# A four-branch mixer layer: the HGRN and GLA tiles issued two at a time, and the mLSTM gate rows in the mixers' banks

## The chip, the cores and the metric

The kernel runs on one core of one Trainium2 chip. The metric is device microseconds of one launch. A core has five engines, each with its own instruction stream that is executed in order: PE multiplies matrices, DVE and POOL do elementwise work and scans, ACT does activations and copies, and SP issues the DMA transfers. An engine waits at the head of its stream until what that instruction needs is there; nothing behind it can pass.

## The reference, cut to what matters

One layer (DEPTH 1) over 2048 tokens of width 1024, in float32: four causal mixers read the same normalised input, and their outputs are gated and summed.

```python
def gla_chunkwise(q, k, v, log_g):      # branches C (HGRN2, 4 heads) and D (GLA, 4 heads)
    ...                                 # chunk by chunk:
    # o = tril(q k^T with decay ratios) v + (q * decay) @ state
    # state = decay_last * state + (k * rest of the decay)^T v
...
def mlstm_chunkwise(q, k, v, log_i, log_f):   # branch B
    ...
    b = jnp.cumsum(fc, axis=-1)
    Dm = jnp.where(mask, b[..., :, None] - b[..., None, :] + ic[..., None, :], -jnp.inf)
...
y = x + (sum over branches of sigmoid(gate_i) * (mixer_i @ W_i)) @ W_out
```

In branches C and D each channel has a decay of its own at each token, so the products between tokens of a chunk can't be one plain matrix product; the kernel builds them level by level (blocks of 8, then 8, 16, 32 and 64 tokens against their neighbours).

## The kernel before, in words

The sequence is worked through in two halves of 1024 tokens. Each half goes through the same stages: the input is normalised and split into high and low parts; `ahead_pairs` runs the large projections (`product`, matmuls at L428) and between them, by the table GORD, the RG-LRU and the mLSTM; `mixers` (L1212) runs the HGRN and GLA recurrences; `merge` and `outp` gate, sum and project the result. In the profiled execution the mixers' stage of the first half lies at about 830 to 1210 us, that of the second at about 2210 to 2580 us.

`mixers` has twelve tiles of 512 tokens: for j in 0 to 3 one HGRN head each, for j = 4 and 5 two GLA heads each, and each j in two parts gi = 0 and 1, the second of which takes up the state S[j] that the first leaves. They are written one after the other, (0,0), (0,1), (1,0) and so on. A tile is the generator `gla_tile` (L977), in eight steps between its `yield`s. It makes a scan Gc of the log decays (L987), an 8-token scan g8 (L989), weights from them (POOL L992, ACT L993 and L994, DVE L995 and L996), the products within blocks of 32 (the 32x32 matmuls of `diag`, L1012, masked at L1020); then for each level of 8, 16, 32 and 64 tokens two POOL subtractions (L1031, L1032), one ACT exponential (L1033), two DVE products (L1034, L1035), and the matmuls (L1012 for the two small levels, L1055 for the two large ones) with their evictions (L1038, L1060). After that come the transposes of the weighted keys (L1078), the state (L1084, L1091), the outputs (L1100, L1104), the norm (ACT L1114 to L1122), transposes back (L1126), the gate product (DVE L1127) and the store (SP, L1130).

PE has other work to do beside the tiles: `ip_vals` (matmuls at L285 into the two banks pb, evicted by ACT at L1145 and DVE at L1147, by DVE at L1149 for the low-rank gate) makes the values that the tiles need, and `gates_ahead` (matmuls at L273) makes merge gates ahead of their time, as many before each tile as the table FILL says. I call the two filler. The weights of filler are split into high and low parts by ACT L254 and POOL L255.

What sets the order: the program is written once, and a scheduler gives each instruction a priority by its place in the program. Tiles are written under `prio(MIX)`, which places them 4000 ahead of filler written at the same place; evictions and weight splits of filler are placed 6000 ahead. The scheduler then lays out each engine's stream with an estimate of its own of when each instruction can start, the highest priority among those ready first. That order is fixed in the program; the chip doesn't change it. Buffers matter too: SBUF slots are handed out by a ring in program order, so that a later tile's slot can be one that an earlier tile has yet to give up. Two ring lists hand out PSUM banks: `bank()` turns over the mixers' banks mx (mx[3:] while the mLSTM runs beside the projections, all six of them in the mixers), `bank8()` those that the projections use (pb and mx[:3] at that time). The mLSTM's gate rows, `mlstm_rows`, take two of their banks (pg, pt) from `bank8()`.

Of the kernel before, what the change touches and what calls it, by code (L numbers as in the profile page):

```python
# [28 lines left out]
NPB = 2  # L29
NG = 10  # L30
PRE = (("mx", 4), ("mo", 4), ("mz", 4), ("hq", 4), ("hz", 4), ("gz", 4), ("gq", 2), ("gk", 2))
LIM = 10
NTH = 0
RMS = 0
NW = 6
NR = 4
# [5 lines left out]
GORD = [('g',2),('r',1),('z',1),('g',1),('z',1),('r',1),('g',1),('z',2),('r',1),('g',1),('z',2),('r',1),('z',6),('t',0),('m',0),('g',1),('m',0),('g',1),('m',0),('c',2),('g',1),('m',0),('c',4),('d',0),('m',0),('c',4),('g',1),('c',5),('g',1),('c',5),('d',1),('c',5),('g',1),('c',5),('g',1),('c',5),('g',1),('c',5),('z',1),('c',4),('z',1),('c',4)]  # L42
NORM = {"hz": "hnw", "gz": "gnw"}
SILU = ("lz", "mz", "hq", "hz", "gz")
FILL = [0, 2, 0, 0, 0, 1, 0, 0, 1, 0, 0, 0, 2, 0]


PV = {}
# [99 lines left out]
class Trunk:  # L148
# [49 lines left out]
    def free(self, *aps):  # L198
        self.ar.free(*aps)

    def run(self, steps):
        for _ in steps:
            pass

    def pbank(self):
        self.bi += 1
# [580 lines left out]
    def mlstm_rows(self, g, temp):  # L787

        nc = self.nc
        V, A = nc.vector, nc.scalar  # L790
        ir = None
        for j in (0, 2):
            ts = [temp() for _ in range(4)]
            for i, t in enumerate(ts):
                nc.sync.dma_start(t[:, :512], self.pdram["xm" if i % 2 else "mx"][j + i // 2][:, g * 512:(g + 1) * 512])
            yield
            pg = self.bank8()
            for i, t in enumerate(ts):
                nc.tensor.matmul(pg[i % 2 * 64:i % 2 * 64 + 36], (self.gx if i % 2 else self.gv)[:, j + i // 2], t[:, :512],
                                 start=(i < 2), stop=(i >= 2))  # L800
            self.free(*ts)
            if ir is None:
                ir = temp()
                A.activation(ir[0:36, :512], pg[0:36], AF.Identity, bias=self.pvt[0:36, PV["mb"][0]:PV["mb"][0] + 1])
            else:
                V.tensor_tensor(ir[0:36, :512], ir[0:36, :512], pg[0:36], op=ALU.add)
            V.tensor_tensor(ir[0:36, :512], ir[0:36, :512], pg[64:100], op=ALU.add)
        lf, m, b, R = (temp() for _ in range(4))
        Pk = lf
        n = 512  # L810
        A.activation(lf[0:4, :n], ir[32:36, :n], AF.Copy)
        V.scalar_tensor_tensor(b[0:4, :n], lf[0:4, :n], -1.0, lf[0:4, :n], op0=ALU.mult, op1=ALU.max)
        A.activation(b[0:4, :n], b[0:4, :n], AF.Exp, scale=-1.0)
        self.ln(b[0:4, :n], b[0:4, :n], bias=1.0)
        V.scalar_tensor_tensor(lf[0:4, :n], lf[0:4, :n], 0.0, b[0:4, :n], op0=ALU.min, op1=ALU.subtract)
        V.tensor_tensor_scan(m[0:4, :n], lf[0:4, :n], ir[0:4, :n], initial=self.mcar, op0=ALU.add, op1=ALU.max)
        V.tensor_tensor_scan(b[0:4, :n], self.cs("r128")[0:4], lf[0:4, :n], initial=0.0, op0=ALU.mult, op1=ALU.add)
        nc.gpsimd.memset(Pk[0:96, :n], 0.0)
        V.tensor_tensor(Pk[0:4, :n], ir[0:4, :n], b[0:4, :n], op=ALU.subtract)
        V.tensor_tensor(R[0:4, :n], b[0:4, :n], m[0:4, :n], op=ALU.subtract)  # L820
        mp = self.mprev[g]
        V.tensor_copy(mp[:, 0:1], self.mcar)
        V.tensor_copy(mp[:, 1:4], m[0:4, 127:383 + 1:128])
        V.tensor_copy(self.mcar, m[0:4, 511:512])

        def c3(t, p0=0):
            return t[p0:p0 + 4, :n].rearrange("p (c t) -> p c t", t=128)

        V.tensor_tensor(c3(R, 32), c3(R), mp.unsqueeze(2).to_broadcast([4, 4, 128]), op=ALU.add)
        A.activation(R[32:36, :n], R[32:36, :n], AF.Exp)  # L830
        V.tensor_tensor(c3(Pk, 32), c3(Pk), c3(R)[:, :, 127:128].to_broadcast([4, 4, 128]), op=ALU.add)
        A.activation(Pk[32:36, :n], Pk[32:36, :n], AF.Exp)
        A.activation(Pk[64:68, :n], m[0:4, :n], AF.Exp, scale=-1.0)
        nc.sync.dma_start(self.rdram[g][0], R[0:4, :n])
        nc.sync.dma_start(self.rdram[g][1], R[32:36, :n])
        pt = self.bank8()
        for c in range(4):
            nc.tensor.transpose(pt[:, c * 96:(c + 1) * 96], Pk[0:96, c * 128:(c + 1) * 128], self.cs("id")[0:96, 0:96])
        cols = self.mcols[g]
        V.tensor_copy(cols, pt[:, 0:384].rearrange("p (c r x) -> p c r x", r=3, x=32)[:, :, :, 0:4])  # L840
        self.free(ir, lf, m, b, R)
# [368 lines left out]


    def mixers(self):  # L1212
        mix = lambda: self.prio(self.MIX)
        self.ahead = 0
        low = NU + 2 * NA
        fill = iter(FILL)
        self.gates_ahead(next(fill))
        hv = self.ip_vals(0, 256)
        steps = [(j, gi) for j in range(6) for gi in range(2)]
        gv, gd, loads = [], [], {}  # L1220

        def load(s):
            j, gi = steps[s]
            if s >= LIM:
                self.ar.base, self.ar.lim = NTH, low
            if j < 4:
                loads[s] = [self.load_p(n, j, gi) for n in ("hq", "hf", "hg")], [self.load_p("hz", j, gi)]
            else:
                loads[s] = ([self.load_p(n, j - 4, gi) for n in ("gq", "gk")],
                            [self.load_p("gz", 2 * j - 8 + i, gi) for i in range(2)])  # L1230

        load(0)
        for s, (j, gi) in enumerate(steps):
            if s == 1:
                hv += self.ip_vals(1, 256)
            elif s == 4:
                gv += self.ip_vals(2, 264, self.lrt[:, :, 0:8])
            elif s == 6:
                self.ar.lim = low
                gv += self.ip_vals(3, 264, self.lrt[:, :, 8:16])  # L1240
                self.ar.lim = None
            elif s == 7:
                with mix():
                    gd = self.gla_decay()
            if s + 1 < len(steps):
                load(s + 1)
            self.gates_ahead(next(fill))
            x, zs = loads.pop(s)
            with mix():
                if j < 4:  # L1250
                    self.run(self.gla_tile(2, gi, [j], *x, [hv[j][gi]], zs, [(0, 128)], self.S[j], self.eps_h))
                else:
                    p = j - 4
                    self.run(self.gla_tile(3, gi, [2 * p, 2 * p + 1], *x, gd[p][gi], [v[gi] for v in gv[2 * p:2 * p + 2]], zs,
                                       [(0, 64), (64, 64)], self.S[j], self.eps_g))
        self.ar.base, self.ar.lim = 0, None


# [296 lines left out]
```

## Time and profile before

| what | us |
|---|---|
| runs of the kernel | 2792.31, 2793.39, 2804.7 (median 2793.39) |
| the profiled execution | 2792.61 |
| its span in the profile | 2790.8 |
| PE busy in the span | 2601.2 |
| mixers' stages of both halves | 750 (830 to 1210 and 2210 to 2580) |

An engine's busy time is the time in which it executes an instruction; a matmul that waits for its operand at the head of PE's stream leaves PE idle. The profile says of each idle stretch what released it. PEclk, or the granted clock, is the share of TensorE's full speed that was granted: its two levels are 1.2 and 2.4 GHz, so that 0.91 over a stretch is a mixture of the two.

### The profile page before, as it was taken

To read this page: it belongs to the slowest core of one execution; us is meant where nothing else is said; L and a number is where in the kernel's file an instruction comes from. 1 tells how busy PE (TensorE), PEld (TensorE's weight loads), DVE (VectorE), ACT (ScalarE), POOL (GpSimd) and SP (SyncE) were. 2 spreads that over 40 slices of the span, in tenths; PEclk is the share of its full clock that TensorE was granted. 3 is DMA by queue.
4 is the path that set the end of the run, shared out by engine and by line. 5 is a ranking of instruction groups with operands and counts; after the bars stand their busy time and mean duration, and the time that the engine had idled before them with its cause. 6 is when DMAs were issued, how large, how long until landed. Compare 5 with 4: busy or idle time off the path is not lost.

```text
span 2790.8 us, 45738 instructions
## 1 busy us (share of the span) xinstructions
PE 2601.2 (93%) x16800; PEld 2154.8 (77%) x16800; DVE 1787.2 (64%) x2907; ACT 1301.7 (47%) x2771; POOL 1506.4 (54%) x1273
## 2 busy tenths in 40 slices
PE   7899999999999798999999999999899897989999
PEld 5677778777888776678977787787788787767789
DVE  7787676676776577633475967766876764875342
ACT  5455445444544454552454454454544443556323
POOL 4566556434446474457465565554354663743763
PEclk9999999999999998999999999999999998999999
DMA  6233224443462235784432332244435523258731
GB/s 220 73 115 114 83 87 144 150 139 116 159 202 77 78 101 191 246 308 142 157 129 84 139 110 87 87 148 137 147 124 164 167 81 103 87 198 304 253 109 72
DMA packets 227072, 393.03 MB, mean 141 GB/s; under 512 B 20720, under 2 KB 78080, under 8 KB 226848
## 3 DMA queue, kind: packets, MB, share of 16 engines
q1 hardware_dynamic: 226848, 390.11, 42.1%
q8 instruction: 132, 2.16, 0.3%
q14 instruction: 92, 0.75, 0.1%
HBM read 270.42 MB, written 119.60 MB: 140 GB/s over the span
## 4 chain that ended last, share of the span: by engine, by line
PE 69%; DVE 10%; DMA 5%; POOL 4%; issue 4%; ACT 3%; SPq 0%; POOLq 0%; DVEq 0%; ACTq 0%
PE mx L428 28%; PE pb L273 13%; PE pb L428 11%; PE pb L285 7%; POOL wl L423 1%; PE mx L285 1%; PE mx L1100 1%; PE mx L1012 1%; PE mx L1104 1%; DMA ob<-in_x_dram 1%; DMA y<-arena 1%; PE mx L1055 1%; PE mx L1126 1%; PE mx L1084 1%; DVE arena L1035 1%
## 5 line engine op out<-in xcount | busy, mean ns | idle before, releaser
L423 POOL TENSOR_TENSOR wl<-wr,wh 128x512 fp32r<-128x512 f32 x264 | 371.6, 1413 | 333.0 <-ACT wh L422 322.8
L423 POOL TENSOR_TENSOR wl<-gth,wh 128x512 fp32r<-128x512 f32 x198 | 289.5, 1463 | 291.6 <-ACT wh L422 281.2
L255 POOL TENSOR_TENSOR wl<-wr,wh 128x512 fp32r<-128x512 f32 (+1 forms) x176 | 246.7, 1409 | 303.6 <-ACT wh L254 222.0
L428 PE MATMUL mx<-s,wh 128*128 128x512 f32 x1104 | 353.0, 399 | 8.8 <-DVE s L311 4.3
L428 PE MATMUL mx<-hh,wh 128*128 128x512 f32 x776 | 310.2, 400 | 11.4 <-DVE mcols L840 4.0
L428 PE MATMUL mx<-hh,wl 128*128 128x512 f32 x776 | 310.2, 400 | 6.3 <-POOL wl L423 6.3
L428 PE MATMUL mx<-hl,wh 128*128 128x512 f32 x776 | 310.1, 400 | 3.2 <-DVE hl L311 3.2
L273 PE MATMUL pb<-hh,wh 128*128 128x512 f32 x704 | 290.0, 414 | 16.3 <-DVE gth L1325 5.4
L437 DVE TENSOR_TENSOR arena<-arena,mx 128x512 f32<-128x512 f32 x346 | 227.2, 679 | 116.4 <-PE mx L428 100.4
L273 PE MATMUL pb<-hl,wh 128*128 128x512 f32 x704 | 290.7, 413 | 0.1
L273 PE MATMUL pb<-hh,wl 128*128 128x512 f32 x704 | 288.4, 410 | 0.4 <-issue 0.4
L285 PE MATMUL pb<-wh,hh 128*128 128x256 f32 (+1 forms) x880 | 255.9, 292 | 15.0 <-DVE arena L1147 9.5
L422 ACT ACTIVATE wh<-wr 128x512 fp32r<-128x512 f32 x264 | 164.1, 625 | 220.3 <-PE mx L428 118.7
L285 PE MATMUL pb<-wl,hh 128*128 128x256 f32 (+1 forms) x880 | 255.3, 290 | 1.8 <-POOL wl L255 1.8
L285 PE MATMUL pb<-wh,hl 128*128 128x256 f32 (+1 forms) x880 | 256.0, 291 | 0.0
L428 PEld LDWEIGHTS mx<-s,wh 128*128 128x128 f32 x1104 | 208.2, 189 | 60.1 <-DVE s L311 7.3
L422 ACT ACTIVATE wh<-gth 128x512 fp32r<-128x512 f32 x198 | 124.1, 627 | 234.4 <-DVE gth L433 162.7
L428 PE MATMUL mx<-s,wl 128*128 128x512 f32 x552 | 217.1, 397 | 0.0
L254 ACT ACTIVATE wh<-wr 128x512 fp32r<-128x512 f32 (+1 forms) x176 | 110.7, 630 | 160.1 <-PE pb L273 103.4
L428 PEld LDWEIGHTS mx<-hh,wh 128*128 128x128 f32 x776 | 148.1, 191 | 47.1 <-ACT wh L422 4.6
L285 PEld LDWEIGHTS pb<-wh,hh 128*128 128x128 f32 x880 | 171.0, 195 | 16.6 <-DVE arena L1147 9.9
L428 PEld LDWEIGHTS mx<-hh,wl 128*128 128x128 f32 x776 | 147.6, 190 | 44.1 <-POOL wl L423 10.9
(494 smaller groups left out, 6296.8 us busy)
## 6 DMA issues: line engine op xcount, KB each, us to landing
wr<-in_wc_dram SPq DMA_DIRECT2D x246, 256.0 KB, 2.8
g<-arena SPq DMA_DIRECT2D x52, 512.0 KB, 3.8
gth<-in_wc_dram SPq DMA_DIRECT2D x66, 256.0 KB, 2.7
wr<-in_wb_dram SPq DMA_DIRECT2D x64, 256.0 KB, 3.0
hl<-y SPq DMA_DIRECT2D x32, 512.0 KB, 5.8
arena<-g SPq DMA_DIRECT2D x46, 256.0 KB, 5.2
arena<-in_xT_dram SPq DMA_DIRECT2D x32, 256.0 KB, 4.7
lw<-g SPq DMA_DIRECT2D x32, 256.0 KB, 5.2
```

The lines of the kernel that those rows point to most:

```text
L254: nc.scalar.activation(hi, raw, AF.Copy)
L255: nc.gpsimd.tensor_tensor(lo, raw, hi, op=ALU.subtract)
L273: nc.tensor.matmul(ps, w[:, ws], h[:, ts], start=(k == 0 and i == 0), stop=(k == nk - 1 and i == 2))
L285: self.nc.tensor.matmul(v, h[:, cs], w[:, ws], start=(first and i == 0), stop=(last and i == 2))
L422: A.activation(hi, w, AF.Copy)
L423: G.tensor_tensor(lo, w, hi, op=ALU.subtract)
L428: nc.tensor.matmul(ps, wp[:, ws], xp, start=(k == 0 and i == 0), stop=(k == 3 and i == 2))
L437: V.tensor_tensor(o, x, y, op=ALU.add)
L1012: T.matmul(ps[b * 32:(b + 1) * 32, c * 32:(c + 1) * 32], wk[p0:p0 + K, s0:s0 + 32], wq[p0:p0 + K, s0:s0 + 32], start=True, stop=True)
L1035: V.tensor_tensor(v4(w)[:, :, 1], v4(w)[:, :, 1], v4(qs)[:, :, 1], op=ALU.mult)
L1055: T.matmul(ps[s0:s0 + m, c * m:(c + 1) * m], w[p0:p0 + K, o:o + m], w[p0:p0 + K, o + m:o + 2 * m], start=True, stop=True)
L1084: T.matmul(pds[p0:p0 + K, c * 128:(c + 1) * 128], kd[:, c * 128 + p0:c * 128 + p0 + K], v[:, cc], start=True, stop=True)
```

## The change

It has two parts. In `mixers` the twelve tiles become six rounds of two tiles that don't depend on each other, (0,0) with (1,0), then (0,1) with (1,1), and so on. The new helper `turns` takes one step of the first, one step of the second, the next step of the first, until both have ended, so that the steps of the two stand alternately in the program. Loads of the tiles' inputs, `ip_vals`, `gla_decay` and the gates of filler are laid by rounds; the table FILL gets new numbers, and LIM and NTH go. In `mlstm_rows` the two banks pg and pt now come from `bank()`.

```diff
-    def run(self, steps):
-        for _ in steps:
-            pass
+    def turns(self, gens):
+
+        while gens:
+            gens = [g for g in gens if next(g, self) is not self]
...
-FILL = [0, 2, 0, 0, 0, 1, 0, 0, 1, 0, 0, 0, 2, 0]
+FILL = [2, 0, 1, 1, 2, 0]
...
-            pg = self.bank8()
+            pg = self.bank()
...
-        pt = self.bank8()
+        pt = self.bank()
...
-        self.gates_ahead(next(fill))
         hv = self.ip_vals(0, 256)
-        steps = [(j, gi) for j in range(6) for gi in range(2)]
+        rounds = [[(j, gi), (j + 1, gi)] for j in (0, 2, 4) for gi in range(2)]
...
-        for s, (j, gi) in enumerate(steps):
-            if s == 1:
+        for r, js in enumerate(rounds):
+            if r == 1:
                 hv += self.ip_vals(1, 256)
-            elif s == 4:
+            elif r == 2:
                 gv += self.ip_vals(2, 264, self.lrt[:, :, 0:8])
-            elif s == 6:
-                self.ar.lim = low
+            elif r == 3:
                 gv += self.ip_vals(3, 264, self.lrt[:, :, 8:16])
-                self.ar.lim = None
-            elif s == 7:
                 with mix():
                     gd = self.gla_decay()
-            if s + 1 < len(steps):
-                load(s + 1)
+            if r < 4:
+                load(r + 1)
             self.gates_ahead(next(fill))
...
+                self.turns([tile(*t) for t in js])
+            if r == 4:
+                self.ar.base, self.ar.lim = 0, low
+                load(5)
```

How many instructions each engine gets is the same but on ACT, which has four more loads of an activation table (41 for 37). Their order differs. Three places follow; in the changed kernel the lines from about L200 on have a number smaller by one (L1011 there is L1012 before). "x16" stands for sixteen like instructions in a row.

The first place is PE in the first half's HGRN tiles. Before, around the end of the third tile, (1,0) (L1126: transposes of its output; mx and pb: banks; arena, ma and mb: slots in SBUF; wh, wl, hh, hl: high and low parts of weights and input):

```order
L285 MATMUL pb_99<-wh_87,hh_70 128x264
L1126 MATMUL mx_101<-cst,arena 128x128
L285 MATMUL pb_99<-wl_93,hh_70 128x264
L1126 MATMUL mx_101<-cst,arena 128x128
L285 MATMUL pb_99<-wh_87,hl_78 128x264
L1012 MATMUL mx_103<-arena 32x32 x16
L1012 MATMUL mx_104<-ma_0_5780 32x32 x16
L1055 MATMUL mx_105<-ma_0_5780 32x32 x8
L1055 MATMUL mx_100<-ma_1_5781 64x64 x4
```

Now, around the end of the same tile, the second of the first round:

```order
L1125 MATMUL mx_104<-cst,arena 128x128
L284 MATMUL pb_98<-wh_83,hh_69 128x256
L284 MATMUL pb_98<-wl_89,hh_69 128x256
L284 MATMUL pb_98<-wh_83,hl_77 128x256
L284 MATMUL pb_98<-wh_83,hh_70 128x256
L1011 MATMUL mx_100<-ma_2_5782,ma_3_5783 32x32 x2
L1125 MATMUL mx_104<-cst,arena 128x128
L1011 MATMUL mx_100<-ma_2_5782,ma_3_5783 32x32 x14
L1011 MATMUL mx_103<-mb_2_5789 32x32 x16
L1054 MATMUL mx_101<-arena 64x64 x4
L284 MATMUL pb_98<-wl_89,hh_70 128x256
```

Before, no filler (L285) stands between the last output transpose and the next tile's L1012 and L1055; now filler stands between the transposes, and again right behind the next products.

The second place is DVE. Before, at the end of the third tile (L1127: the gate product that ends a tile; L987: the scan that opens one):

```order
L1127 TENSOR_TENSOR arena<-mx_101,arena 128x512
L987 SCALAR_TENSOR_TENSOR arena<-cst,mb_2_5789 128x512
L1071 COPY egl_202<-ma_1_5781 128x4
L1072 TENSOR_TENSOR ma_1_5781<-ma_1_5781,mb_1_5788 128x512
L1034 TENSOR_TENSOR arena<-arena,mb_2_5789 128x32x8
L1035 TENSOR_TENSOR arena<-arena,mb_1_5788 128x32x8
L1034 TENSOR_TENSOR ma_0_5780<-ma_0_5780,mb_2_5789 128x16x16
L1035 TENSOR_TENSOR ma_0_5780<-ma_0_5780,mb_1_5788 128x16x16
```

Now, at the end of the first round (L1126 and L986 in its numbering):

```order
L1126 TENSOR_TENSOR mb_1_5788<-mx_103,mb_1_5788 128x512
L1037 COPY_PREDICATED ma_0_5780<-cst,mx_101 128x128
L1070 COPY egl_201<-arena 128x4
L1071 TENSOR_TENSOR arena<-arena,mb_4_5791 128x512
L1126 TENSOR_TENSOR mb_3_5790<-mx_104,mb_3_5790 128x512
L1019 TENSOR_TENSOR mb_0_5787<-mx_100,cst 128x128
L1037 COPY_PREDICATED ma_0_5780<-cst,mx_103 128x128
L986 SCALAR_TENSOR_TENSOR mb_2_5789<-cst,arena 128x512
L1087 COPY arena<-S_180 128x128
L1059 COPY arena<-mx_101 64x4x64
```

Before, the next scan stands right behind the gate product of the tile before and takes the slot that this tile's output leaves when it has been stored; only that tile's own next rows follow. Now the gate products of both tiles of the round have rows of other tiles between them and the next scan, and this scan takes another slot (mb_2, not mb_1 or mb_3).

The third place is PE in the first half's GLA tiles, where filler is the gates' L273 (L272 now). Before, around the 32-token level of the first of them:

```order
L273 MATMUL pb_99<-hh_70,wl_90 128x512
L273 MATMUL pb_98<-hl_78,wh_84 128x512
L273 MATMUL pb_98<-hh_70,wl_90 128x512
L1055 MATMUL mx_105<-arena 32x32 x8
L1055 MATMUL mx_100<-arena 32x32 x8
L273 MATMUL pb_99<-hh_67,wh_85 128x512
L273 MATMUL pb_99<-hl_75,wh_85 128x512
```

Now, around that level of the first two:

```order
L272 MATMUL pb_98<-hh_68,wl_92 128x512
L1125 MATMUL mx_104<-cst,mb_2_5789 128x128
L1011 MATMUL mx_102<-arena 32x32 x16
L1011 MATMUL mx_101<-ma_3_5783 32x32 x16
L1011 MATMUL mx_103<-mb_0_5787 32x32 x9
L1011 MATMUL mx_104<-ma_2_5782 32x32 x16
L1011 MATMUL mx_102<-ma_3_5783 32x32 x16
L1011 MATMUL mx_103<-mb_0_5787 32x32 x7
L1054 MATMUL mx_105<-mb_0_5787 32x32
L1054 MATMUL mx_100<-mb_0_5787 32x32
```

Before, the level stands among gate matmuls; now six groups of products of the tiles follow upon each other, and a gate matmul comes only after 39 rows.

## Rows read from the trace of the kernel before

**Rows 1.** Page, part 1: each engine's busy time, share of span, instructions.

```profile
PE 2601.2 (93%) x16800; PEld 2154.8 (77%) x16800; DVE 1787.2 (64%) x2907; ACT 1301.7 (47%) x2771; POOL 1506.4 (54%) x1273
```

**Rows 2.** Page, part 4: the chain that ended last, by engine.

```profile
PE 69%; DVE 10%; DMA 5%; POOL 4%; issue 4%; ACT 3%; SPq 0%; POOLq 0%; DVEq 0%; ACTq 0%
```

**Rows 3.** Stretches: length, busy PE, PEld, DVE, ACT, POOL, granted clock, DMA share, GB/s.

```profile
500.00:830.00 330.00, 315.88 (x1596) 258.10 (x1595) 229.33 (x445) 149.95 (x351) 144.10 (x118) 0.98 0.46 148
830.00:1000.00 170.00, 141.54 (x1623) 131.60 (x1623) 104.30 (x197) 69.17 (x180) 97.52 (x106) 0.91 0.28 92
1000.00:1210.00 210.00, 187.74 (x2015) 145.96 (x2016) 133.94 (x244) 120.57 (x305) 103.81 (x105) 0.90 0.57 194
...
2000.00:2210.00 210.00, 199.48 (x1031) 167.39 (x1030) 156.06 (x299) 99.20 (x244) 95.43 (x77) 0.97 0.48 152
2210.00:2400.00 190.00, 158.17 (x1841) 146.58 (x1840) 119.78 (x228) 77.27 (x207) 110.93 (x120) 0.93 0.27 87
2400.00:2580.00 180.00, 163.11 (x1792) 125.35 (x1791) 121.88 (x209) 106.09 (x274) 90.06 (x91) 0.91 0.64 220
```

**Rows 4.** PE's waits, 830 to 1000: us in total, times, longest.

```profile
PE mx L1012 <- DVE arena L1035: 8.5, 2, 8.0
PE pb L285 <- DVE arena L1147: 4.7, 1, 4.7
PE mx L1012 <- DVE mb L1035: 4.3, 2, 3.8
```

**Rows 5.** PE's waits, 2210 to 2400.

```profile
PE mx L1012 <- DVE arena L1035: 9.6, 3, 8.0
PE mx L1012 <- DVE mb L1035: 5.9, 2, 5.4
```

**Rows 6.** PE's waits, 1000 to 1210, and (last row) 500 to 830.

```profile
PE mx L1126 <- ACT ma L1122: 8.1, 2, 4.8
...
PE mx L838 <- ACT arena L832: 4.4, 1, 4.4
```

**Rows 7.** Timeline, both halves: start, us, engine, line, operation, [idle before <-releaser].

```profile
916.59 5.62 POOL L255 TENSOR_TENSOR wl<-wr,wh 128x528 fp32r<-128x528 f32 x4
...
917.96 0.28 PE L285 MATMUL pb<-wh,hl 128*128 128x264 f32 x1
...
918.08 0.28 PE L285 MATMUL pb<-wh,hh 128*128 128x264 f32 x1
...
918.30 1.55 DVE L1035 TENSOR_TENSOR arena<-arena 128x256 f32<-128x256 f32 x1
...
925.23 0.59 PE L285 MATMUL pb<-wh,hh 128*128 128x264 f32 x1 [4.72 <-DVE arena L1147]
...
925.61 0.42 PE L285 MATMUL pb<-wl,hh 128*128 128x264 f32 x1
...
925.83 0.42 PE L285 MATMUL pb<-wh,hl 128*128 128x264 f32 x1
...
930.26 0.69 DVE L1127 TENSOR_TENSOR arena<-mx,arena 128x512 f32<-128x512 f32 x1 [5.08 <-PE mx L1126]
...
933.04 1.23 DVE L987 TENSOR_TENSOR_SCAN arena<-cst,mb 128x512 f32<-128x512 f32 x1 [2.10 <-DMA y<-arena]
...
937.41 0.83 DVE L1035 TENSOR_TENSOR arena<-arena,mb 128x256 f32<-128x256 f32 x1
...
938.39 0.66 PE L1012 MATMUL mx<-arena 128*32 128x32 f32 x32 [8.05 <-DVE arena L1035]
...
2307.22 0.59 PE L285 MATMUL pb<-wh,hh 128*128 128x264 f32 x1 [4.73 <-DVE arena L1147]
```

**Rows 8.** Instructions of L1035 and L1031: ns min/median/max, first and last start.

```profile
L1035 DVE TENSOR_TENSOR arena<-arena x28: 406/828/1547, 899.4 to 2525.2; 128x256 f32<-128x256 f32 x28
...
L1031 POOL TENSOR_TENSOR ma<-arena x30: 608/791/1784, 840.5 to 2411.7; 128x256 f32<-128x256 f32 x30
```

**Rows 9.** Groups of ACT by line: busy us, mean ns of one, idle before.

```profile
L232 ACT ACT_TABLE_LOAD x6 | 7.7, 1283 | 0.1
```

More of the change, by code (lines that the diff above doesn't have):

```diff
@@ L31 @@
 PRE = (("mx", 4), ("mo", 4), ("mz", 4), ("hq", 4), ("hz", 4), ("gz", 4), ("gq", 2), ("gk", 2))
-LIM = 10
-NTH = 0
 RMS = 0
@@ L1216, in mixers, with load @@
         fill = iter(FILL)
-        self.gates_ahead(next(fill))
         hv = self.ip_vals(0, 256)
-        steps = [(j, gi) for j in range(6) for gi in range(2)]
+        rounds = [[(j, gi), (j + 1, gi)] for j in (0, 2, 4) for gi in range(2)]
         gv, gd, loads = [], [], {}
[L1222 to L1225, printed above, removed]
+        def load(r):
+            for j, gi in rounds[r]:
+                if j < 4:
+                    loads[j, gi] = [self.load_p(n, j, gi) for n in ("hq", "hf", "hg")], [self.load_p("hz", j, gi)]
+                else:
+                    loads[j, gi] = ([self.load_p(n, j - 4, gi) for n in ("gq", "gk")],
+                                    [self.load_p("gz", 2 * j - 8 + i, gi) for i in range(2)])
@@ L1226, in load, with tile @@
+        def tile(j, gi):
+            x, zs = loads.pop((j, gi))
             if j < 4:
[L1227 to L1230, printed above, removed]
+                return self.gla_tile(2, gi, [j], *x, [hv[j][gi]], zs, [(0, 128)], self.S[j], self.eps_h)
+            p = j - 4
+            return self.gla_tile(3, gi, [2 * p, 2 * p + 1], *x, gd[p][gi], [v[gi] for v in gv[2 * p:2 * p + 2]], zs,
+                                 [(0, 64), (64, 64)], self.S[j], self.eps_g)
@@ L1243, in mixers @@
                 with mix():
                     gd = self.gla_decay()
-            if s + 1 < len(steps):
-                load(s + 1)
+            if r < 4:
+                load(r + 1)
             self.gates_ahead(next(fill))
-            x, zs = loads.pop(s)
             with mix():
[L1250 to L1255, printed above, removed]
+                self.turns([tile(*t) for t in js])
```

## The prediction

> **What bounds the kernel now.** I read the busy times first [rows 1]: PE is busy for 2601.2 of 2790.8 us, and 69% of the chain that ended last is PE [rows 2]. So only two things can move the time by much: PE standing idle (190 us in all), and PE's granted clock. Then the stretches [rows 3], to see where the idle time is. In the four rows of the mixers' stages PE is idle for 170 - 141.5 = 28.5, 210 - 187.7 = 22.3, 190 - 158.2 = 31.8 and 180 - 163.1 = 16.9 us, 99.5 of the 190 us in 750 us of the span. In the two rows in which the mLSTM runs beside the projections it is 14.1 and 10.5 us. The granted clock in the mixers' rows is 0.90 to 0.93; in the mLSTM's it is 0.97 and 0.98.
>
> Then PE's waits in those stretches [rows 4, 5]. In the six HGRN tiles or so that lie in the first stretch of each half, nearly all are for DVE: for the level product L1035 (8.5 and 4.3 us, 9.6 and 5.9 us) or for an eviction of filler, L1147 (4.7 us in the first half, and 4.73 in the second [rows 7]). The 3.8 of the 4.3 and 5.4 of the 5.9 us are the start of the stage, where no tile stands ahead. The timeline around 930 us [rows 7] shows where the longest, 8.05 us, comes from. The third tile's gate product waits for its transposes (930.26, L1127); the next scan waits for the store of that tile's output (933.04, L987, 2.10 behind a DMA), since it takes the same slot; then POOL, ACT and DVE go through the fourth tile's first level (L1035 at 937.41), and only then PE has something to do. The order of before shows why nothing covers it: on PE the L1012 and L1055 of that tile stand right behind the last transpose, with no filler between.
>
> **What the change does, part by part.** The sum is made against the profiled execution, 2792.6 us (span 2790.8 and 1.8 around it), which lies 0.8 below the median of the runs. The counts of instructions are the same on every engine but ACT, so PE's work at full clock is the same; what can change is how much of it stands still.
>
> *Two tiles in turn, HGRN.* In the order now, the products of a tile have those of another, independent tile and filler between their steps. I counted in both orders the places at which a product of a tile follows, with less than some 2 us of other PE work, on what its operands hang on: 36 rows in 12 groups in the first half and 34 in 10 in the second before, 20 in 7 and 19 in 6 now; in the first six tiles, two groups are left. Of the scans that hang on a y store of a tile just ended, three a half before, one is left. The price of these places is in rows 3 to 5. Without the two starts (3.8 and 5.4, which stay, since both first tiles begin with the same scan, POOL step and exponential) the idle time of the two stretches is 24.7 + 26.4 = 51.1 us. Of it I take back: all waits on arena L1035, 8.5 + 9.6 = 18.1; one half of those on L1147, 4.7, because DVE's levels now stand in longer rows ahead of some evictions; and one third of the rest (51.1 - 18.1 - 9.4 = 23.6), 7.9. Together **-30.7**. Bounds: all of it, -51, and nothing, 0.
>
> *Two tiles in turn, GLA.* Here two tiles of two heads each make four heads at once on six banks. PE's idle time in these stretches is 22.3 + 16.9 = 39.2 us, the longest row being the transposes L1126 that wait for ACT's L1122, 8.1 us [rows 6]. The order now has a run of 39 rows of L1011 and L1054 with no gate matmul, which gives less cover there, and alternating steps, which give more. I take **0**. Bounds: -15 (the L1122 waits and half of what is left in that stretch) to +39 (the idle time doubles).
>
> *FILL and the place of filler.* The same filler is spread over other places; as much of it lies behind the last output transpose as before (row 4294 before, 4307 now, of some 11,100). One run of 290 rows of filler lies ahead of the last HGRN round, whose slots wait for `gla_decay` and thus for `ip_vals`: PE is busy there and DVE is not, so it costs nothing by itself, but that filler is then missing elsewhere. It is in the +39 above; no term of its own.
>
> *The clock.* The timeline [rows 7] shows filler matmuls starting 0.12 us apart (917.96, 918.08) and, right behind the wait of 4.72 us, 0.22 us apart (925.61, 925.83): the lower of the two levels. A stretch with granted clock c has run 2(1 - c) of its length at half speed, and half of that is lost: (1 - 0.91) x 170 + (1 - 0.93) x 190 = 15.3 + 13.3 = 28.6 us in the first stretches, 0.10 x 210 + 0.09 x 180 = 37 in the second. The low level lay behind a wait there, and three fifths of the first stretches' waits go (30.7 of 51.1); small 32-column products stay where they are, so I take only a third of 28.6, **-10**. Bounds: 0 to -28.
>
> *Table loads.* Four more on ACT, 1.283 us each [rows 9], 5.1 us. ACT is busy for 69 to 121 us of the mixers' stretches [rows 3]: **0**. If they come in front of an L1122 that PE waits for, up to +5.
>
> *Gate rows in the mixers' banks.* pg and pt now come out of mx[3:], beside the mLSTM's own score banks, and leave the projections' five banks alone. PE's order there is the same up to the gate rows and agrees again behind them; between, some groups of products have changed places with L798 and L837. The largest row is PE's 4.4 us behind L832 [rows 6]; the projection that waited with it may no longer, but the ring of three is fuller. I take **-2**; bounds from the nearest rows, -8 (that wait, and as much in the second half) to +8 (such a wait more in each half, for a bank that a gate row holds while its chain ends).
>
> Sum: -30.7 + 0 - 10 + 0 - 2 = -42.7, so 2792.6 - 42.7 = 2749.9, **2750 us**.
>
> **Rivals.**
> *Given back.* The waits go from the HGRN tiles and come again where the cover is thinner: in the run without gate matmuls, and at evictions behind the rows of levels. For it: the total of filler is the same, and PE's idle time in the GLA stretches doubled is +39, which nearly cancels -42.7. Against: far fewer tight places in the order in both halves. It gives 2792.6 - 42.7 + 39 = 2789.
>
> *Slower: DVE and POOL in each other's way.* One level product takes 0.41 us at the least, 0.83 in the middle and 1.55 at most [rows 8]. The timeline shows when: 0.83 us beside POOL's subtractions of the same level, 1.55 beside POOL's splits L255 (918.30, POOL busy from 916.59 on) [rows 7]. Two tiles in turn put one tile's L1031 beside the other's L1035 all the time. If the 96 L1035 (28 of them in the row shown, in seven such rows) and 96 L1034 go up by 0.45 us each, DVE has 86 us more to do; its busy time in the four stretches is 104 + 134 + 120 + 122 = 480 of 750 us, so it is free for a third of the time; I let 0.6 of the extra hide beside PE's filler, and 0.4 x 86 = 35 comes to the end; POOL's L1031, 0.61 to 1.78, goes the same way. With nothing gained that gives 2827. It decides from the point at which the mean of L1035 is above some 1.2 us. Against: DVE and POOL are at six tenths of these stretches, and there was overlap of two tiles before. The Trainium skill (SBUF — State Buffer, Who interferes with whom) says that a DVE instruction with two SBUF inputs contends with a GpSimd instruction that reads SBUF; by that rule all 192 products are open to it, and the trace's steps of 0.41, 0.83 and 1.55 us agree. By the rule taken alone the time would be this rival's 2827, by the rows above the forecast's 2750.
>
> *More than forecast.* All 51 us of waits go and the clock's 28 with them: 2792.6 - 51 - 28 - 2 = 2712.
>
> *The change doesn't do what it says*: the scheduler could have put the tiles back one behind the other. The order shows that it hasn't; no chance of its own.
>
> **How the numbers follow.** Chances: forecast 0.55, given back 0.20, slower 0.15, more than forecast 0.10. The forecast's own range, with half of the bounds of its terms, is 2725 to 2778. The range 2712 to 2812 holds the forecast, given back and most of the larger gain; the slower case lies above it but for its lighter forms. A measurement of this kernel tells about 0.5%, 14 us, from no change. Faster by more than that (below 2779): 0.55 + 0.10 and little else, 0.65. Within: 0.18, nearly all of given back. Slower: 0.15 and 0.02 of given back, 0.17.
>
> **What would show it.** If right: PE idle in 830 to 1000 and 2210 to 2400 at about 13 and 16 us in place of 28.5 and 31.8, no wait of 8 us on L1034 (L1035 before), a granted clock of 0.93 to 0.95 there; GLA stretches as before; 500 to 830 within 4 us of before. If given back: these waits gone, and PE's idle time and the rows of waits on L1121, L1125 and L1146 grown from about 1000 us on. If slower: a median of L1034 above 1.2 us, and DVE's busy time in the stage up by some 40 us a half. What would make the forecast wrong first is a row of DVE's order that the trace runs later than the scheduler thought, with an eviction of filler behind it: then both PE's filler and the tile wait.

## The result, and the profile after

The changed kernel takes 2764.99 us, the median of four runs (2763.77 to 2767.64), where the kernel before takes 2799.05 us on the same chip (2792.31 to 2809.4): a ratio of 0.9876, 95% interval 0.9839 to 0.9914. It is faster, by 34 us (1.2%) in the medians. The profiled executions are nearer to each other, since that of before was one of its quicker ones: spans of 2790.8 and 2762.8 us, 28.0 apart. Forecast were 2750 us and 42.7 us of gain, with a range of 2712 to 2812.

The page of the changed kernel, busy time of each engine (the row that answers to [rows 1]); PE does the same work, in a shorter span:

```profile
PE 2594.8 (94%) x16800; PEld 2152.5 (78%) x16800; DVE 1769.8 (64%) x2907; ACT 1305.2 (47%) x2775; POOL 1514.3 (55%) x1273
```

[Rows 3] were cut at round times. To find where 28 us went, the cuts have to lie at the same work, so I cut both traces at the first and the last matmul of the values (`ip_vals`) and at the first matmul of the output projection after `merge`. I call the first piece the values' stretch (the HGRN tiles lie beside it), the second the rest of the stage (the GLA tiles and `merge`). The kernel before, stretches of both halves; columns as in [rows 3] (length, busy PE, PEld, DVE, ACT, POOL, granted clock, DMA share, GB/s):

```profile
826.60:1024.30 197.70, 169.24 (x1905) 156.93 (x1905) 124.25 (x238) 81.24 (x214) 116.36 (x126) 0.92 0.28 90
1024.30:1310.20 285.90, 261.29 (x2174) 202.47 (x2173) 148.41 (x244) 140.06 (x320) 163.06 (x144) 0.92 0.65 222
2206.70:2405.50 198.80, 166.97 (x1905) 154.40 (x1904) 126.27 (x238) 81.27 (x215) 118.36 (x125) 0.93 0.28 91
2405.50:2680.10 274.60, 255.80 (x2173) 199.59 (x2172) 149.73 (x245) 133.54 (x316) 161.14 (x145) 0.94 0.64 221
```

The changed kernel, the same work:

```profile
828.70:1002.90 174.20, 162.05 (x1845) 149.26 (x1844) 124.91 (x230) 80.50 (x214) 112.76 (x120) 0.96 0.33 109
1002.90:1295.40 292.50, 262.96 (x2234) 207.97 (x2234) 145.78 (x253) 139.08 (x319) 168.72 (x150) 0.91 0.63 216
2191.40:2363.60 172.20, 159.88 (x1845) 147.21 (x1844) 123.54 (x227) 80.48 (x215) 114.24 (x120) 0.98 0.34 111
2363.60:2652.10 288.50, 257.20 (x2235) 203.61 (x2234) 149.82 (x256) 138.53 (x319) 166.82 (x150) 0.93 0.62 208
```

The values' stretch is 23.5 and 26.6 us shorter, the rest of the stage 6.6 and 13.9 us longer. Up to the first stage the changed kernel is 2.1 us later, between the stages 0.5 quicker: 2.1 - 23.5 + 6.6 - 0.5 - 26.6 + 13.9 = -28.0. PE's idle time (length less busy) in the values' stretch goes from 28.5 and 31.8 to 12.1 and 12.3 us, and the clock from 0.92 and 0.93 to 0.96 and 0.98. In the rest of the stage idle time grows from 24.6 and 18.8 to 29.5 and 31.3, and the clock goes from 0.92 and 0.94 to 0.91 and 0.93. Sixty matmuls of tiles (1905 to 1845, 2174 to 2234) have moved from the first piece to the second, but PE's busy time there rose by only 1.7 and 1.4 us, so that most of what the second lost is idle time. The sum over both pieces is what counts.

PE's waits of the changed kernel, 820 to 1000 us (where [rows 4] stand for before): the waits of 8.0 and of 4.7 us are gone, and no single wait there is longer than 2.6 us.

```profile
PE mx L1011 <- DVE arena L1034: 3.8, 3, 2.6
PE mx L1103 <- DVE arena L1090: 2.4, 3, 1.3
PE mx L1054 <- DVE arena L1034: 2.1, 1, 2.1
```

The instructions of L1034, which was L1035 in [rows 8], in the changed kernel: its two largest groups; columns: busy us, mean ns, idle before.

```profile
L1034 DVE TENSOR_TENSOR arena<-arena 128x256 f32<-128x256 f32 x24 | 20.3, 845 | 0.0
L1034 DVE TENSOR_TENSOR arena<-arena,mb 128x256 f32<-128x256 f32 x22 | 18.2, 826 | 0.0
```

All 96 of L1034 add up to 69.7 us, 726 ns each, where the 96 of L1035 before add up to 76.6 us, 798 ns each.

### The profile page after: what moved, and what is told of

Its sections match the earlier page's. It is cut to its first block, busy times and chain, and to the rows that moved or that the text cites. A ratio compares the mean times of both kernels' runs of the same rounds, so it can differ in the third digit from the quotient of the medians.

```text
span 2762.8 us, 45749 instructions
## 1 busy us (share of the span) xinstructions
PE 2594.8 (94%) x16800; PEld 2152.5 (78%) x16800; DVE 1769.8 (64%) x2907; ACT 1305.2 (47%) x2775; POOL 1514.3 (55%) x1273
## 5 line engine op out<-in xcount | busy, mean ns | idle before, releaser
L254 POOL TENSOR_TENSOR wl<-wr,wh 128x512 fp32r<-128x512 f32 (+1 forms) x176 | 255.1, 1460 | 213.5 <-ACT wh L253 186.3
L272 PE MATMUL pb<-hh,wh 128*128 128x512 f32 x704 | 293.6, 418 | 19.9 <-DVE lw L1324 7.1
L272 PE MATMUL pb<-hl,wh 128*128 128x512 f32 x704 | 289.5, 411 | 2.6 <-DVE hl L1298 2.6
L272 PE MATMUL pb<-hh,wl 128*128 128x512 f32 x704 | 286.1, 407 | 0.0
L272 PEld LDWEIGHTS pb<-hh,wh 128*128 128x128 f32 x704 | 139.1, 198 | 57.8 <-DVE lw L1324 9.2
L427 PEld LDWEIGHTS mx<-hh,wl 128*128 128x128 f32 x776 | 146.8, 189 | 44.1 <-POOL wl L422 10.6
```

Of the source, the lines that this page charges most:

```text
L254: nc.gpsimd.tensor_tensor(lo, raw, hi, op=ALU.subtract)
L272: nc.tensor.matmul(ps, w[:, ws], h[:, ts], start=(k == 0 and i == 0), stop=(k == nk - 1 and i == 2))
L427: nc.tensor.matmul(ps, wp[:, ws], xp, start=(k == 0 and i == 0), stop=(k == 3 and i == 2))
```

## The experiments

All ratios are to the kernel before, with their 95% intervals; "idle" is PE's idle time in the values' stretch of the first and of the second half.

### Which of the two parts

`mix_only` is the changed kernel without the change in `mlstm_rows`, `rows_only` the kernel before with that change alone (the diff is that of `rows_only`).

```diff
             yield
-            pg = self.bank8()
+            pg = self.bank()
...
-        pt = self.bank8()
+        pt = self.bank()
```

> The changed kernel with the gate rows' banks pg and pt back in the projections' ring; the mixers' part alone. Theory: the mixers' part carries all of the gain, and the bank change cost about 1.5 us (the stage began 2.0 us later in the first half of the profiled run, the second half was 0.5 shorter up to there): a span of about 2761 for 2763, the first stage beginning at 826 to 827 us, ratio to before 0.987. Rival: the bank change brings part of the gain: span 2770 or more.

> The kernel before with only the gate rows' banks taken from the mixers' ring. Theory: within 3 us of before (span 2788 to 2794), with the wait of 4.4 us of L838 replaced by another of the same size (6.7 us in the changed kernel). Rival, the bank change is worth something by itself: span 2783 or less, the first mixers' stage beginning 3 us earlier or more.

Measured: `mix_only` 2772.2 us, 0.9906 (0.9891 to 0.9922), idle 15.9 and 15.2; `rows_only` 2781.06 us, 0.994 (0.9922 to 0.9959). So the mixers' part makes most of the gain, and both of my theories on the banks failed (about 2761 us for `mix_only`, 2788 to 2794 for `rows_only`): alone, the bank change is worth 0.4 to 0.8%. Of its mechanism the traces show this much. Late in the second half's mLSTM, 1960 to 2190 us, the kernel before has these two waits of PE:

```profile
PE mx L428 <- DVE mcols L840: 3.7, 1, 3.7
PE mx L428 <- ACT arena L443: 3.7, 1, 3.7
```

A projection group (L428) gets the bank in which the gate rows' pt lies, and waits until L840 has copied it out. `rows_only` has one wait in their place:

```profile
PE mx L428 <- DVE arena L437: 3.5, 1, 3.5
```

In the traces of before, `mix_only`, `order_only`, `loads_only`, `hold_z` and `hold2`, all with the old banks, the two waits stand, 3.7 to 5.7 us behind L840 and 3.6 to 4.2 behind L443; in the eight with the new banks neither is among the largest, and the wait behind L437 (3.2 to 4.3) is. That is some 4 us. In the first half nothing is won: the wait of 4.4 us of L838 [rows 6] goes, and this one comes (changed kernel, 480 to 830 us; in `rows_only` it is 6.7 us as well):

```profile
PE mx L919 <- DVE arena L901: 6.7, 1, 6.7
```

The 18.5 us by which `rows_only`'s median lies below that of before are more than these 4 us. The profiled runs of before and `rows_only` are 5.7 us apart (spans 2790.8 and 2785.1). Over all fourteen traces the time outside the two mixers' stages points the same way: 1824 to 1830 us in seven of the eight with the new banks and 1834 to 1837 in five of the six with the old ones, some 7 us less. The two exceptions are the changed kernel itself (1835.4) and `mix_only` (1828.3). The rest stays open, and the same change on top of `hold_z` (below) gave nothing in the medians.

### Is it the turn-taking

`seq` writes the two tiles of a round one after the other, all else as changed:

```diff
-                self.turns([tile(*t) for t in js])
+                for t in js:
+                    self.turns([tile(*t)])
```

`gla_seq` does that in the last two rounds only. `dep_pairs` keeps the turns, but pairs (j,0) with (j,1), of which the second needs the state of the first; `dep_seq` is `dep_pairs` with its tiles one after the other, that is, the old sequence of tiles under the new rounds:

```diff
-        rounds = [[(j, gi), (j + 1, gi)] for j in (0, 2, 4) for gi in range(2)]
+        rounds = [[(j, gi) for gi in range(2)] for j in range(6)]
```

> The changed kernel, rounds, loads and FILL as they are, but the two tiles of a round written one after the other instead of step by step in turn. Theory (the turn-taking fills PE's waits): PE's idle time from the first filler matmul of the stage to the last returns from 12 to about 28 us in each half, with one wait of 8 us or so again, span about 2790. Rival (what helps is the new sequence, in which neighbours don't share state and slots, and the filler's new places): idle time there at 12 to 16, span 2763 to 2770.

> The changed kernel with turn-taking in the four HGRN rounds only; the GLA tiles of the last two rounds are written one after the other. Theory (part of the gain is given back because four heads in turn stand without gate matmuls between them): the stretch from the last values' matmul to the end of the last tile goes from 180.5 and 181.5 us to about 176 and 171, span 2750 to 2757. Rival (that stretch is longer because some 60 matmuls of tiles and the wait for the slots moved into it, whatever its order): 2760 to 2768.

> The changed kernel, but the two tiles of a round are (j,0) and (j,1), of which the second takes up the first one's state; step by step in turn, filler and FILL at the same rounds. If independence of the two matters, the stretch of the values returns to 185 us or more (from 174 and 172) and the span to 2780 or more; if it is the slots and the filler, 2758 to 2770.

> The changed kernel's loads, FILL, slots and banks by rounds, with the tiles in the old sequence, (0,0), (0,1), (1,0), one after the other: what is left of the mixers' part without its pairs. If the loads and slots by rounds carry the gain, 2758 to 2772; if the pairs do, 2780 or more, with a wait of some 8 us in the stretch of the values.

Measured: `seq` 2762.64 us, 0.9874 (0.9856 to 0.9891); `gla_seq` 2777.11, 0.992 (0.9904 to 0.9937); `dep_pairs` 2774.18, 0.9927 (0.9914 to 0.994); `dep_seq` 2756.81, 0.9863 (0.9846 to 0.988). The values' stretches of `seq`:

```profile
826.30:1002.10 175.80, 159.94 (x1805) 146.65 (x1805) 120.23 (x226) 80.39 (x213) 109.99 (x115) 0.97 0.33 108
2184.70:2358.80 174.10, 159.14 (x1805) 146.81 (x1804) 121.71 (x225) 81.03 (x213) 113.29 (x115) 0.97 0.33 111
```

and of `dep_seq`:

```profile
825.40:998.10 172.70, 158.61 (x1805) 145.57 (x1804) 122.81 (x225) 80.06 (x213) 111.00 (x115) 0.98 0.33 110
2176.00:2350.20 174.20, 160.86 (x1805) 148.51 (x1804) 123.26 (x224) 80.86 (x213) 111.62 (x115) 0.95 0.33 110
```

My theory fell here. Without any turn-taking the idle time stays at 15.9 and 15.0 us, and with neither turns nor independent pairs at 14.1 and 13.3; the times are equal to the changed kernel's or below. With dependent pairs, turns are slower than no turns: 0.9927 against 0.9863, intervals apart. The loss is not where I expected it: the values' stretches of `dep_pairs`, 174.4 and 171.5 us long, are as short as the changed kernel's, its rests are longer (299.4 and 296.8 us against 292.5 and 288.5). `gla_seq` missed its theory too: taking the turns out of the GLA rounds alone didn't get back what these lost. Its median lies 12 us above that of the changed kernel, with intervals that still overlap; from `seq`, which ran on the same chip, they are apart.

### What it was

Left were the sequence of the tiles, the places of the loads and with them the slots, and the places of the filler, which the next three runs leave as before. `order_only` is the kernel before with the new sequence, one tile at a time; `loads_only` is the kernel before with the inputs of two tiles loaded together, a round ahead, and those of the last two tiles behind the tenth, as in the changed kernel (cut to the main lines, as is the next diff):

```diff
+        load(1)
...
-            if s + 1 < len(steps):
-                load(s + 1)
+            if s % 2 == 0 and s < 8:
+                load(s + 2)
+                load(s + 3)
...
```

`hold_z` is the kernel before with one thing altered: the slot of a tile's gated output goes back to the ring only when the next tile has taken the slots of its two scans, so that no scan gets it.

```diff
         Gc, g8 = self.T(), self.T()
+        self.free(*self.held)
+        self.held = []
...
-        self.free(q, k, g, *vs, *zgs)
+        self.free(q, k, g, *vs)
+        self.held = list(zgs)
...
```

> The kernel before with one edit: the slot in which a tile leaves its gated output is given back to the ring only after the next tile has taken its two scan slots, so that no scan waits for the store of the tile just ended. Order of the tiles, FILL and banks as before. Theory (the waits of 8 us and their like come from that slot): no wait of 8 us behind L1035's successor, PE idle from the first to the last matmul of the values down from 28 to 32 us to 12 to 18 in each half, span about 2765, ratio 0.990. Rival (the wait is one of tiles whose neighbours share a state, or of filler in the wrong place): idle there stays above 24, span 2783 or more.

> The kernel before with only the sequence of its tiles changed to that of the rounds, (0,0), (1,0), (0,1), (1,1) and so on, one at a time; loads, LIM, FILL and banks as before. If independent neighbours are what helps, span 2765 or less with 12 to 18 us of idle PE in the stretch of the values; if the slots or the filler's places are, 2783 or more.

> The kernel before with only the tiles' input loads issued by rounds of two, as in the changed kernel (which also moves the slots that later tiles get); tiles in the old sequence and one at a time, FILL, LIM's place by round, banks as before. Theory (the loads by rounds change which slots the ring hands out, and the scans no longer wait for a y store): PE idle in the stretch of the values 12 to 18 us, that stretch at 172 to 180, span 2755 to 2770. Rival (it is the places of the values' projections by rounds): idle there stays above 24, span 2785 or more.

Measured: `order_only` 2794.84 us, 0.9988 (0.9972 to 1.0003), no change; `loads_only` 2772.25, 0.991 (0.9885 to 0.9935); `hold_z` **2740.93, 0.9808** (0.9791 to 0.9825), better than both kernels and 24 us below what I expected of it. `loads_only` gives what the whole mixers' part of the change gives (`mix_only`, 0.9906). The values' stretches of `order_only`, as idle as before (31.4 and 30.3 us):

```profile
829.10:1028.40 199.30, 167.93 (x1905) 155.43 (x1904) 126.53 (x237) 81.04 (x214) 118.50 (x125) 0.92 0.28 90
2203.80:2403.90 200.10, 169.76 (x1905) 157.07 (x1904) 128.06 (x237) 81.22 (x214) 116.62 (x125) 0.91 0.27 90
```

Of `loads_only`, 13.8 and 15.7 us idle:

```profile
828.00:1010.90 182.90, 169.10 (x1957) 153.39 (x1956) 134.43 (x253) 88.04 (x237) 125.64 (x130) 0.98 0.32 107
2190.40:2373.80 183.40, 167.67 (x1949) 153.90 (x1948) 131.64 (x248) 86.06 (x235) 121.83 (x130) 0.95 0.32 106
```

Of `hold_z`, its values' stretches and the rests of its stages:

```profile
826.60:1013.40 186.80, 170.24 (x1989) 155.93 (x1988) 138.31 (x254) 89.79 (x240) 126.45 (x130) 0.96 0.31 101
1013.40:1276.70 263.30, 247.09 (x2092) 195.42 (x2091) 140.64 (x228) 126.14 (x290) 159.04 (x140) 0.96 0.70 237
2176.70:2362.90 186.20, 170.59 (x1989) 156.41 (x1988) 136.68 (x254) 89.75 (x240) 127.02 (x130) 0.96 0.31 102
2362.90:2635.70 272.80, 252.42 (x2091) 197.82 (x2090) 140.03 (x228) 124.80 (x290) 157.56 (x140) 0.94 0.64 218
```

DVE's waits for a store, 820 to 1025 us, in the kernel before:

```profile
DVE arena L987 <- DMA y<-arena: 6.9, 2, 4.8
```

and in `order_only`:

```profile
DVE arena L987 <- DMA y<-arena: 6.6, 2, 4.5
```

In `order_only` PE's wait of 8 us stands as well:

```profile
PE mx L1012 <- DVE arena L1035: 9.7, 3, 8.0
```

In the kernel before, ACT and POOL stand idle with PE until the scan of 933.04 us [rows 7] is done:

```profile
934.30 0.63 ACT L1069 ACTIVATE ma<-arena 128x512 f32<-128x512 f32 x1 [12.16 <-DVE arena L987]
...
934.35 0.61 POOL L1031 TENSOR_TENSOR arena<-arena 128x256 f32<-128x256 f32 x1 [12.14 <-DVE arena L987]
```

In `loads_only`, `hold_z` and the changed kernel no scan waits for a store there. (In `seq` and `dep_seq` DVE does wait for one, 3.2 us, but at L1087, the copy of a state.) So the waits of 8 us, one in each half, come from the ring: before, it hands a tile's first scan the slot from which the tile before has still to store its output, and everything of the new tile stands behind that store. Of the 8.05 us only 2.10 are the wait for the store; the rest is the old tile's gate product ahead of it and the new tile's scan and first level behind it. What a wait for a store costs depends on the cover: the longest, 4.8 us in the kernel before, falls where filler stands, and no wait of PE in the ten us behind it is longer than 1.5. The waits of 4.7 us for L1147 are of another kind. In the first half DVE works without a gap from 914 us until that eviction, and no store is waited for; in `hold_z`, with its other order, these waits are gone too, and no run isolates them.

Independent neighbours don't help, as `order_only` shows, since the slot ties them together. `loads_only` hands out other slots, and it also brings the inputs sooner; `hold_z` leaves the loads' places alone, but it too changes which slots everything behind it gets. This also tells why turns aren't needed: once the slots are free, the scheduler overlaps the tiles by itself. On DVE, two scans L987 stand ahead of the first tile's gate product in the order of before and of `order_only`; in `loads_only` it is three, in `seq`, where the tiles are written one after the other, four, and in `hold_z` five.

The loads by rounds also have a price, in the rest of the stage. PE's idle time there, both halves together, is 61 to 73 us in the eight traces that have them (`loads_only` 62.6, `seq` 66.9, the changed kernel 60.8) and 37 to 48 us in the six that keep the loads of before, whatever the sequence, the turns and the banks. No run shows by which wait.

`hold_z` is shorter in the rest of the stage too, by 22.6 and 1.8 us, where the changed kernel is longer. 84 matmuls more than before run beside the values (1989 against 1905), where the changed kernel has 60 fewer, and that leaves less for the GLA rounds. It is not the whole reason, and no run isolates it: `loads_only` also has some 50 more beside the values, and its second half's rest is 287.2 us, longer than before.

Three more variants of it. `after_hold` is the changed kernel with the slots of a round held back in this way, `hold_rows` is `hold_z` with the new banks, and `hold2` is `hold_z` that holds each slot for one tile more:

```diff
-        self.free(*self.held)
-        self.held = []
+        if len(self.held) > 1:
+            self.free(*self.held.pop(0))
```

> The changed kernel with the gated outputs' slots of a round held back until both tiles of the next round have taken their scan slots. If the slots were all that the mixers' part of the change mended, nothing is left to gain in the stretch of the values (174 and 172 us stay) and the time is 2757 to 2766; if the two add up (the GLA stretch of the changed kernel still waits for slots), 2730 to 2745.

> The kernel before with the gated output's slot held back as in hold_z and, besides, the gate rows' banks from the mixers' ring. If the bank change is worth what it gave by itself (0.994), 2725 to 2733; if it was a matter of the mixers' stage that hold_z mends anyway, 2738 to 2744, as hold_z.

> As hold_z, but each tile's output slot is held back until the tile after the next has taken its scan slots. In hold_z POOL still waits for a y store (the memset at L1003, 41.7 us in 4 times in the whole run, 12.3 us the longest). Theory (those waits are off PE's path, since POOL is not what PE waits for there): within 8 us of hold_z, 2733 to 2749. Rival (every wait for a y store in the stage costs): the stage's idle PE falls from 33 and 36 us a half to 25 or less and the time is below 2730.

Measured: `after_hold` 2768.0 us, 0.989 (0.9871 to 0.9909); `hold_rows` 2746.62, 0.9815 (0.9791 to 0.9839); `hold2` 2763.18, 0.9874 (0.9852 to 0.9897). `after_hold` lies 2 us above what I expected if the changed kernel had already mended the slots: the hold adds nothing to it, and its values' stretches stay at 172.9 and 171.7 us. By the medians the bank change adds nothing to `hold_z`, and `hold_rows` lies above both of the ranges that I gave; its profiled run is the shorter of the two, though (spans 2740.0 and 2746.4), so a few us either way stay open. `hold2` missed both expectations and is 22 us slower than `hold_z` in the medians, 10.5 in the profiled runs. (The longest of the memset's waits in `hold_z` is 13.3 us, not 12.3.) Its values' stretch is as good (13.5 us idle in the first half), but in the rest of that stage PE is idle for 27.3 us where it was 16.2, and the largest wait in it, 1010 to 1190 us, is for a norm:

```profile
PE mx L1128 <- ACT arena L1124: 10.5, 2, 8.3
```

The clock there is 0.93 against 0.96. Other slots gave the scheduler another order, and this one has a gap that the other has not; that part isn't a law of slots, and I have no run that takes it further.

## Why the prediction was right or wrong

**HGRN tiles, -30.7: right in size, wrong in cause.** The values' stretches lost 35.8 us of idle time (16.3 and 19.5); 16.1 of them are the two waits of 8 us. The two starts, which I had left in place at 3.8 and 5.4 us, gave some too: PE's longest wait there is now 2.6 us. What I read from [rows 7] held: the scan in the slot of the output just stored, then POOL, ACT and DVE, then PE. The step that failed is the one behind it, "in the order now, the products of a tile have those of another, independent tile and filler between their steps". I saw in the order that the next scan takes another slot, and laid the gain to the turns all the same. `seq` and `dep_seq` have the shorter stretches without turns; `loads_only` and `hold_z` have them in the old sequence, one tile at a time.

**GLA tiles, 0, and no term for `merge`: here the size failed.** PE's idle time in the rest of the stage rose by 4.9 and 12.5 us, 17.4 in all: 2.0 and 7.9 up to the last tile's end, 2.9 and 4.6 in `merge` behind it. That is the rival "given back", at somewhat under half of the +39 that I priced it at, and not by its mechanism: without turns the idle time there is no smaller (`seq` 34.1 and 32.8 us, `dep_seq` 31.2 and 35.5, against 29.5 and 31.3), and `loads_only`, with the old sequence and filler, has 29.0 and 33.6. It came with the loads by rounds, for which I had no term. Over both pieces PE's idle time fell by 11.4 + 7.0 = 18.4 us.

**The clock, -10: right in the sum, wrong in both of its places.** By (1 - c) times the length of the whole stage, the time lost at the lower level fell from 38.7 and 28.4 us to 32.7 and 23.0, by 11.4. By the rows cut at the values, it fell from 29.7 to 10.4 us in the values' stretches, by nearly two thirds where I took one third (c is 0.96 and 0.98 there, not 0.93 to 0.95); no run shows the reason that I gave for the third. In the rest of the stage, where I had nothing, it rose from 39.4 to 46.5. That the two together make about the -10 is luck. Besides, this reckoning counts the lower level in PE's idle time too, which the idle terms count already. Counted in the traces only while PE was busy, the values' stretches lose 10.6 us less than before and the rests 5.3 us more.

**Gate rows, -2: wrong for want of a row.** I priced them from the first half, where one wait took the place of another (the stage begins 2.1 us later in the changed kernel, 0.8 sooner in `rows_only`). The two waits of 3.7 us in the second half stood in the trace of before, and I didn't see that a projection was waiting for just the bank that the change gives back. By itself this part is worth 0.4 to 0.8%.

**Table loads, 0, and FILL, 0:** nothing in the runs speaks against them, and none isolates them.

The parts add up to the 28.0 us by which the spans differ: idle -18.4, the lower clock while PE was busy -5.3, PE's busy time reckoned at full clock -5.9 (801.8 to 795.9 us in the two stages; no run tells why), outside the stages +1.6 (1833.8 to 1835.4). Of the forecast's -42.7, 12 us are missing in the idle time: the first piece gained 5 more than forecast, and the second gave back 17. The slower rival fell: the mean of the level product went down, from 798 to 726 ns, not up towards 1.2 us; no more of them met POOL's splits than before (14 of 96 in both), and 31 ran with no POOL instruction beside them, at 0.41 to 0.42 us, where 17 did before.

## What to carry to other kernels

When a step waits for a DMA that stores somebody else's result, look at which buffer they share before giving the code another order: holding one slot back for a little while was worth more here than the whole rewrite in pairs. Such a wait cost PE 8 us where nothing covered it and left no wait above 1.5 us where filler stood. The scheduler of this kernel, which goes by readiness, interleaved independent work by itself; what it couldn't do is undo a choice of buffer made in program order. And price a stage as a whole, since a stretch that sheds its waits may only have handed its cover, or its work, on to the next one.

## What was not expected of the hardware

One account fits all 28 mixers' stages of the fourteen traces: the stage's length less PE's idle time, less (1 - c) times its length, is 386 to 402 us, while the lengths go from 450 to 485 (c being the granted clock). What differs between these orders is idle time (31 to 56 us) and time lost at the lower clock (18 to 44 us), and what is left agrees to within some 2% either way, in whatever order PE's matmuls stand. Two per cent of 394 us is still 8 us, a good part of what is argued about here, and the highest values are those of `hold_z` and `hold_rows`, which have the least of both: idle time at the lower level is taken off twice. With the lower level counted only while PE is busy (16 to 32 us), what is left is 396 to 403 us in all 28 stages, within 1% either way.
